# Two made token sums loaded and split in the mixers' temporary tiles, and product 2 of the last up step put last

## The chip, the cores and the metric

One core of one Trainium2 chip runs one launch of the kernel. The metric is the device time of that launch in microseconds, the median of three runs. In the profile, PE is the matrix engine (PEld its weight loads), DVE the vector engine, ACT the scalar engine, POOL and SP two more engines which here mainly issue DMA transfers, each through a queue of its own that works in order.

## The reference

A decoder layer on 2048 tokens of width 1024, all in float32: three kinds of gated token mixers, an output projection into the residual, then an MLP with a causal convolution of width 3.

```python
def conv_ffn(h, w_up, conv_w, conv_b, w_down):
    u = h @ w_up                                   # 1024 -> 2 * 2816
    u = lax.conv_general_dilated(u, ..., feature_group_count=2 * D_FF) + conv_b
    val, gate = jnp.split(u, 2, axis=-1)
    return (jax.nn.silu(gate) * val) @ w_down      # 2816 -> 1024

def reference(x, c, ...):
    ...
        h = rms_norm(x) * (1.0 + sc1) + sh1
        x = x + g1 * token_mixer(h, w_in[l], ..., w_out[l], pos)
        h = rms_norm(x) * (1.0 + sc2) + sh2
        x = x + g2 * conv_ffn(h, w_up[l], conv_w[l], conv_b[l], w_down[l])
    return rms_norm(x) * final_gain
```

## The kernel before

**Numbers.** Every float32 product is made of three matmuls on rounded parts: an operand is split into a high part (a cast on ACT, L1006) and a low part (a subtraction on DVE, L1007) by `split`, and `split3` (L239 to L241) adds high x high, high x low and low x high into one PSUM bank.

**Stages.** The mixers and the output projection go over 4 blocks `b` of 512 tokens. A block's output projection comes in two halves (`out_half`), each of four pieces of weights (`out_piece`, tiles hwo and lwo with block, half and piece in the name); its results are added to the residual x (L953), whose squares (sqn, san) are summed by eight small matmuls (ssn) and brought back to all partitions by eight more (bcn) for the norm n2. The MLP follows in 2 stages `s` of 1024 tokens. The up-projection of a stage (`up_stage`) takes 22 steps `f`, each 128 columns of the value half and of the gate half. A step is one 2 x 2 block product in the form of Winograd and Strassen with 7 products instead of 8: operand A_i comes from the weights, B_i from the tokens, i = 1 to 7. `product(ps, A, B, i, first)` is 4 k-tiles of three matmuls, so 12 matmuls of 128 x 512.

**The order of a step.** `up_first` runs products 1 (bank X), 2 (Y), 6 (X), 5 (Z), 7 (X); ACT copies bank X after 1 (m1), 6 (u2) and 7 (u3), DVE adds Y and Z to uv and ug. `up_second` runs 4 (X) and 3 (Z). Between products 1 and 2 of a step stands `up_second` of the step before, so that copies of X and work of PE overlap; behind the last step `up_second` stands alone.

**The token operands.** B_1, B_2 and B_3 are split from the tokens themselves (hr), B_6, B_5, B_7 and B_4 from sums which `early_sums` makes in DRAM (`made`) while the last block's mixers run. `fetch_made` loads a sum's four k-tiles through POOL into the four `t2k` buffers of the pool "gemm" (tiles hm) and splits them. That pool takes the space that the mixers' pools leave when they are closed. `tmp` gives one of the mixers' six temporary tiles `te`; the split parts of B_7 also live there.

**The weight operands.** A step's A_i are split from loads of up weights (r00, r01, r11: row half and column half) and of their sums (s1 to s4) into the ring `W4` of 1024-wide tiles, which cycles through the buffers that also serve the output weights: whi (3), wlo (3) and wraw (2). The two first products of step 0 of stage 0 are `begun` before the mixers' end, from one 128 x 1024 load (rv0).

**What sets the order.** PE's order is the program's. Other work around it is put into that order by a clock of estimated PE time (`clock.at`): a norm's broadcast is due `gap` after its sums. DVE, ACT, SP and POOL are ordered by a scheduler from the program and its priorities (`tc.high_priority`): each engine then works in order, and an instruction that waits holds up all behind it.

## Time and profile before

| | us |
|---|---|
| median of 3 runs | 2538.81 |
| lowest, highest | 2534.95, 2539.82 |
| the profiled execution | 2537.37 |
| its span | 2535.6 |
| PE busy in it | 2489.7 |
| DVE, ACT, POOL busy | 1949.3, 1136.8, 152.1 |

The span runs from the first to the last instruction that the profile shows. The mean clock granted to PE was 0.992 of the full one. A row of the timeline gives start, duration, engine, line, operation and tiles, and in brackets how long the engine had been idle before it and what released it. Buffer and step numbers are left out in tile names of the profile: X<-B,A is a product of any step.

### The profile page before, as it was taken

What the parts mean: (1) busy time and instruction counts of PE and PEld (TensorE: products, weight loads), DVE (VectorE), ACT (ScalarE), POOL (GpSimd) and SP (SyncE); (2) the same over time, 40 slices, a digit from 0 to 9 for tenths busy, and PEclk for the clock granted to TensorE, in tenths of its full rate; (3) what the DMA queues carried; (4) which work ended last, traced back from release to release, by engine and by line L of the source; (5) the groups of instructions that cost most, each with busy time, mean ns of one, the idle gap of its engine ahead of it and who ended that gap; (6) DMA issues with size and microseconds to landing.
All of it is one profiled execution on the core that took longest, in us unless ns stands there. A gap on an engine that the chain in (4) does not pass through costs nothing.

```text
span 2535.6 us, 37063 instructions
## 1 busy us (share of the span) xinstructions
PE 2489.7 (98%) x13175; PEld 2114.7 (83%) x13175; DVE 1949.3 (77%) x3566; ACT 1136.8 (45%) x1913; POOL 152.1 (6%) x271
## 2 busy tenths in 40 slices
PE   7999999999999999999999999999999999999998
PEld 6898888888789888988788888888877888888887
DVE  8787976869678776868788888877678777778666
ACT  4443434433434335333455554455445545555542
POOL 1000000000000000000100000000001010010000
PEclk9999999999999999999999999999999999999999
DMA  8455575676687846884754544487665544447653
GB/s 295 175 187 175 202 270 209 233 261 215 224 317 266 282 156 240 293 284 142 250 179 149 171 146 145 163 287 240 213 212 169 158 138 153 150 133 259 220 192 126
DMA packets 227930, 524.95 MB, mean 207 GB/s; under 512 B 24952, under 2 KB 28064, under 8 KB 227744
## 3 DMA queue, kind: packets, MB, share of 16 engines
q1 hardware_dynamic: 224544, 512.08, 59.0%
q0 software_dynamic: 3200, 10.49, 1.1%
q8 instruction: 104, 1.70, 0.3%
q14 instruction: 82, 0.67, 0.1%
HBM read 392.97 MB, written 129.50 MB: 206 GB/s over the span
## 4 chain that ended last, share of the span: by engine, by line
PE 58%; DVE 5%; DMA 4%; issue 1%; ACT 1%; SPq 0%; DVEq 0%; ACTq 0%; POOLq 0%
PE X L239 6%; PE X L240 6%; PE X L241 6%; PE Z L240 3%; PE dX L239 3%; PE Z L241 3%; PE dX L240 3%; PE dX L241 3%; PE Z L239 3%; PE Y L239 2%; PE Y L240 2%; PE Y L241 2%; PE dY L239 1%; PE dY L241 1%; PE dY L240 1%
## 5 line engine op out<-in xcount | busy, mean ns | idle before, releaser
L239 PE MATMUL X<-B,A 128*128 128x512 f32 x572 | 223.1, 390 | 1.4 <-ACT u L1285 1.4
L241 PE MATMUL X<-B,A 128*128 128x512 f32 x572 | 222.6, 389 | 0.0
L240 PE MATMUL X<-B,A 128*128 128x512 f32 x572 | 222.6, 389 | 0.0
L1007 DVE TENSOR_TENSOR dA<-rd,dA 128x512 fp32r<-128x512 f32 x154 | 106.0, 688 | 90.5 <-ACT dA L1006 90.1
L1006 ACT CAST dA<-rd 128x512 fp32r<-128x512 f32 x154 | 95.6, 620 | 147.2 <-PE dX L241 62.7
L240 PE MATMUL dX<-dB,dA 128*128 128x512 f32 x396 | 154.3, 390 | 2.7 <-DVE dB L1007 2.7
L239 PE MATMUL dX<-dB,dA 128*128 128x512 f32 x396 | 154.3, 390 | 1.3 <-DVE y L1463 0.9
L241 PE MATMUL dX<-dB,dA 128*128 128x512 f32 x396 | 154.1, 389 | 0.0
L1007 DVE TENSOR_TENSOR A<-s,A 128x512 fp32r<-128x512 f32 x176 | 120.5, 685 | 38.3 <-ACT A L1006 38.1
L239 PE MATMUL psvgh<-hvgh,ha 128*128 128x256 f32 x480 | 141.0, 294 | 0.0
L241 PE MATMUL psvgh<-hvgh,ha 128*128 128x256 f32 x480 | 136.3, 284 | 0.0
L240 PE MATMUL psvgh<-lvgh,ha 128*128 128x256 f32 x480 | 136.2, 284 | 0.0
L1006 ACT CAST A<-s 128x512 fp32r<-128x512 f32 x176 | 108.6, 617 | 53.6 <-PE Z L241 43.5
L239 PEld LDWEIGHTS X<-B,A 128*128 128x128 f32 x572 | 107.4, 188 | 24.4 <-ACT u L1285 2.2
L241 PEld LDWEIGHTS X<-B,A 128*128 128x128 f32 x572 | 107.4, 188 | 22.4
L240 PE MATMUL Z<-B,A 128*128 128x512 f32 x308 | 121.5, 394 | 4.6 <-DVE B L1007 4.6
L240 PEld LDWEIGHTS X<-B,A 128*128 128x128 f32 x572 | 107.4, 188 | 22.2
L643 PE MATMUL lvh<-qbh,kh 128*128 128x128 f32 x896 | 121.9, 279 | 1.5 <-DVE nw L157 1.4
L643 PEld LDWEIGHTS lvh<-qbh,kh 128*128 128x128 f32 x896 | 115.9, 192 | 8.4 <-issue 2.5
L239 PE MATMUL Z<-B,A 128*128 128x512 f32 x308 | 121.0, 393 | 1.2 <-ACT B L1006 1.2
L241 PE MATMUL Z<-B,A 128*128 128x512 f32 x308 | 120.9, 392 | 0.0
L1007 DVE TENSOR_TENSOR dB<-rb,dB 128x512 fp32r<-128x512 f32 x154 | 105.3, 684 | 10.1 <-ACT dB L1006 10.1
(472 smaller groups left out, 6998.9 us busy)
## 6 DMA issues: line engine op xcount, KB each, us to landing
gs<-yv SPq DMA_DIRECT2D x154, 256.0 KB, 2.8
rb<-gs SPq DMA_DIRECT2D x154, 256.0 KB, 4.1
r<-wup SPq DMA_DIRECT2D x141, 256.0 KB, 3.3
s<-sumsu SPq DMA_DIRECT2D x132, 256.0 KB, 3.0
wada<-wada SPq DMA_DIRECT2D x48, 512.0 KB, 4.6
rd<-sumsd SPq DMA_DIRECT2D x88, 256.0 KB, 4.2
rd<-wdown SPq DMA_DIRECT2D x66, 256.0 KB, 3.5
x<-xT SPq DMA_DIRECT2D x64, 256.0 KB, 5.5
```

The source lines that it names most:

```text
L239: T.matmul(ps, lhs[0], rhs[0], start=first, stop=False, skip_group_check=more)
L240: T.matmul(ps, lhs[0], rhs[1], start=False, stop=False, skip_group_check=more)
L241: T.matmul(ps, lhs[1], rhs[0], start=False, stop=last, skip_group_check=more)
L643: T.matmul(ps[:, c * P:(c + 1) * P].rearrange("p (h n s) -> p h n s", h=2, s=s), kq[rs, c * P:(c + 1) * P], rhs, start=True, stop=True)
L1006: S.copy(hi, src)
L1007: V.tensor_tensor(lo, src, hi, op=ALU.subtract)
```

## The change

- The last output piece (block 3, half 1, piece 3) uses the two `wraw` buffers instead of a whi and a wlo.
- The ring `W4` begins with the two `wraw` and then takes whi and wlo in turn; it still has eight places.
- The first up weights come as two 128 x 512 loads (r00, r01) into `te` tiles instead of one into `wraw`.
- Sums 6 and 5 are loaded (`load_made`) right after the first output piece of the last half is begun, into `te` tiles, and split (`split_made`) at a raised priority. Sums 7 and 4 still use `t2k`.
- The due time of the broadcast of the last block's norm n2 goes from 4.5 to 10.0.
- In the last step of either stage product 2 and its sum on DVE (`second`) come behind product 7.
- A parameter `room` is passed through `out_half` and `out_finish`, as None.

```diff
-    def piece(src, name, key, both=False, ahead=50):
+    def piece(src, name, key, both=False, ahead=50, tags=(("whi", 3), ("wlo", 3))):
...
-            hi = pw.tile([P, 1024], F32R, tag="whi", name="h" + name)
-            lo = pw.tile([P, 1024], F32R, tag="wlo", name="l" + name)
+            hi, lo = (pw.tile([P, 1024], F32R, tag=t, name=n + name, bufs=bufs) for n, (t, bufs) in zip("hl", tags))
...
-                     both=True, ahead=250 if (b, half) == (0, 0) else 600 if (b, half) == (NB - 1, 1) else 50)
+                     both=True, ahead=250 if (b, half) == (0, 0) else 600 if (b, half) == (NB - 1, 1) else 50,
+                     tags=[("wraw", NRAW)] * 2 if (b, half, i) == (NB - 1, 1, 3) else (("whi", 3), ("wlo", 3)))
...
-        clock.at(4.0, rstd(acc, f"n2_{b}", bc[:], then if b else lambda: put_off.append(then), gap=8.0 if b < NB - 1 else 4.5))
+        clock.at(4.0, rstd(acc, f"n2_{b}", bc[:], then if b else lambda: put_off.append(then), gap=8.0 if b < NB - 1 else 10.0))
...
-    W4 = [("whi", 3)] * 3 + [("wlo", 3)] * 3 + [("wraw", NRAW)] * 2
+    W4 = [("wraw", NRAW)] * 2 + [("whi", 3), ("wlo", 3)] * 3
...
-    def fetch_made(B, i):
+    def load_made(i, tile):
+        r = []
         for k in range(4):
-            x = t2k(f"hm{i}_{k}")
+            x = tile(f"hm{i}_{k}")
             G.dma_start(x[:], made[i, k][:])
+            r.append(x)
+        return r
+
+    def split_made(B, i, raw):
+        for k, x in enumerate(raw):
             B[i, k] = split(x[:], *hc_tile(f"B0_{i}_{k}"))
...
     with tc.high_priority(offset=300):
-        rv0 = pw.tile([P, 1024], F32, tag="wraw", name="rv0_0", bufs=NRAW)
-        nc.sync.dma_start(rv0[:], wup[0])
         A = {}
-        up_op(A, 0, 0, 1, rv0[:, 0:512])
-        up_op(A, 0, 0, 2, rv0[:, 512:1024])
+        for i in range(2):
+            r = tmp(f"r0{i}_0_0")
+            nc.sync.dma_start(r[:], wup[0][:, 512 * i:512 * i + 512])
+            up_op(A, 0, 0, i + 1, r[:])
...
     with tc.high_priority(offset=100):
         out_begun = [out_begin(NB - 1, 1, 0)]
+        raw6, raw5 = (load_made(i, tmp) for i in (6, 5))
...
-        if not begun:
-            product(Y, A, B, 2, True)
-        with tc.high_priority(offset=HOT):
-            V.tensor_tensor(uv[:, 2:514], Y[:], m1[:], op=ALU.add)
+        def second():
+            if not begun:
+                product(Y, A, B, 2, True)
+            with tc.high_priority(offset=HOT):
+                V.tensor_tensor(uv[:, 2:514], Y[:], m1[:], op=ALU.add)
+        if f < NF - 1:
+            second()
...
             V.tensor_tensor(ug[:, 514:SB + 2], Z[:], u3[:], op=ALU.add)
+        if f == NF - 1:
+            second()
...
-    fetch_made(B, 6)
-    fetch_made(B, 5)
+    with tc.high_priority(offset=100):
+        split_made(B, 6, raw6)
+        split_made(B, 5, raw5)
...
     for i in (7, 4):
-        fetch_made(B, i)
+        split_made(B, i, load_made(i, t2k))
```

POOL's loads of the made sums (hm, sum and k-tile in the name), before:

```order
L1058 DMA hm6_0_12079<-made6_0_9991 128x512
L1058 DMA hm6_1_12084<-made6_1_10301 128x512
L1058 DMA hm6_2_12089<-made6_2_10703 128x512
L1058 DMA hm6_3_12094<-made6_3_11045 128x512
L1265 MEMSET uv0_0_12316 128x2
L1265 MEMSET ug0_0_12317 128x2
L1265 MEMSET uv0_1_12421 128x2
L1058 DMA hm5_0_12099<-made5_0_9988 128x512
L1058 DMA hm5_1_12104<-made5_1_10298 128x512
L1058 DMA hm5_2_12109<-made5_2_10700 128x512
L1058 DMA hm5_3_12114<-made5_3_11042 128x512
L1058 DMA hm7_0_12251<-made7_0_9994 128x512
```

The same twelve places now:

```order
L1059 DMA hm6_0_12040<-made6_0_9991 128x512
L1059 DMA hm6_1_12042<-made6_1_10301 128x512
L1059 DMA hm6_2_12044<-made6_2_10703 128x512
L1059 DMA hm6_3_12046<-made6_3_11045 128x512
L1059 DMA hm5_0_12048<-made5_0_9988 128x512
L1059 DMA hm5_1_12050<-made5_1_10298 128x512
L1059 DMA hm7_0_12253<-made7_0_9994 128x512
L1059 DMA hm7_1_12255<-made7_1_10304 128x512
L1059 DMA hm7_2_12257<-made7_2_10706 128x512
L1059 DMA hm5_2_12052<-made5_2_10700 128x512
L1059 DMA hm5_3_12054<-made5_3_11042 128x512
L1059 DMA hm7_3_12259<-made7_3_11048 128x512
```

The loads of sum 5 move ahead of the three memsets, and three of sum 7 ahead of sum 5's last two.

DVE around the end of the last mixer (oTr) and the first sum of step 0 (uv), ahead of the last block's residual updates (x1), before:

```order
L1278 TENSOR_TENSOR uv0_0_12316<-Y0_0_11989,m1_0_0_12320 128x512
L587 SCALAR_TENSOR_TENSOR oTr3_1_12043<-oTr3_1_12038,vec_84,oTr3_1_12043 128x512
L1007 TENSOR_TENSOR B0_6_0_12081<-hm6_0_12079,B0_6_0_12081 128x512
L1007 TENSOR_TENSOR B0_6_1_12086<-hm6_1_12084,B0_6_1_12086 128x512
L953 SCALAR_TENSOR_TENSOR x1_3_0_11636<-y3_1_0_12018,mod_102,x1_3_0_11636 128x512
L953 SCALAR_TENSOR_TENSOR x1_3_0_11636<-y3_1_1_12019,mod_102,x1_3_0_11636 128x512
L953 SCALAR_TENSOR_TENSOR x1_3_2_11751<-y3_1_2_12050,mod_102,x1_3_2_11751 128x512
L953 SCALAR_TENSOR_TENSOR x1_3_2_11751<-y3_1_3_12051,mod_102,x1_3_2_11751 128x512
```

Now:

```order
L1286 TENSOR_TENSOR uv0_0_12318<-Y0_0_11991,m1_0_0_12322 128x512
L1007 TENSOR_TENSOR B0_6_0_12097<-hm6_0_12040,B0_6_0_12097 128x512
L1007 TENSOR_TENSOR B0_6_1_12100<-hm6_1_12042,B0_6_1_12100 128x512
L1007 TENSOR_TENSOR B0_6_2_12103<-hm6_2_12044,B0_6_2_12103 128x512
L1007 TENSOR_TENSOR B0_6_3_12106<-hm6_3_12046,B0_6_3_12106 128x512
L1007 TENSOR_TENSOR B0_5_0_12109<-hm5_0_12048,B0_5_0_12109 128x512
L1007 TENSOR_TENSOR B0_5_1_12112<-hm5_1_12050,B0_5_1_12112 128x512
L586 SCALAR_TENSOR_TENSOR oTr3_1_12061<-oTr3_1_12056,vec_84,oTr3_1_12061 128x512
L1007 TENSOR_TENSOR lB0_7_0_12262<-hm7_0_12253,hB0_7_0_12261 128x512
L1007 TENSOR_TENSOR B0_5_2_12115<-hm5_2_12052,B0_5_2_12115 128x512
```

Eight low parts of sums (L1007) stand ahead of the residual updates instead of two; the third and fourth of sum 6 and all of sum 5 stood behind them.

SP's loads for the last half's output pieces (hwo, lwo) and the first up steps (r, s), before:

```order
L223 DMA lwo3_1_0_12015<-kepto4l_3461 128x1024
L223 DMA lwo3_1_1_12047<-kepto5l_3522 128x1024
L222 DMA hwo3_1_0_12014<-kepto4h_3459 128x1024
L223 DMA lwo3_1_2_12150<-kepto6l_3577 128x1024
L222 DMA hwo3_1_1_12046<-kepto5h_3520 128x1024
L222 DMA hwo3_1_2_12149<-kepto6h_3575 128x1024
L1199 DMA s1_0_0_12192<-sumsu0_11589 128x512
L1199 DMA s0_0_0_12191<-sumsu0_11589 128x512
L1138 DMA r11_0_0_12207<-wup 128x512
L1138 DMA r00_0_1_12383<-wup 128x512
L1138 DMA r01_0_1_12385<-wup 128x512
L1138 DMA r11_0_1_12409<-wup 128x512
```

Now:

```order
L1119 DMA r00_0_0_11980<-wup 128x512
L1119 DMA r01_0_0_11985<-wup 128x512
L221 DMA hwo3_1_0_12016<-kepto4h_3459 128x1024
L222 DMA lwo3_1_0_12017<-kepto4l_3461 128x1024
L221 DMA hwo3_1_1_12064<-kepto5h_3520 128x1024
L222 DMA lwo3_1_1_12065<-kepto5l_3522 128x1024
L221 DMA hwo3_1_2_12151<-kepto6h_3575 128x1024
L222 DMA lwo3_1_2_12152<-kepto6l_3577 128x1024
L221 DMA hwo3_1_3_12189<-kepto7h_3639 128x1024
L222 DMA lwo3_1_3_12190<-kepto7l_3641 128x1024
L1206 DMA s1_0_0_12194<-sumsu0_11589 128x512
L1206 DMA s0_0_0_12193<-sumsu0_11589 128x512
```

The output pieces stand together, the last of them now ahead of the first sums of up weights (s1, s0) instead of behind them, and the two loads of the first up weights stand at the head.

More of the change, by code (lines that the diff above doesn't have):

```diff
@@ L939, in out_begin, with out_half @@
         return wp, pss
-    def out_half(b, half, acc=None, after_pieces=None, begun=()):
+    def out_half(b, half, acc=None, after_pieces=None, begun=(), room=None):
         for i in range(4):
@@ L955, in out_half, with out_finish @@
                     with tc.high_priority(offset=HOT):
-                        sumsq(acc, x1[m], m, f"n2_{b}_")
+                        sumsq(acc, x1[m], m, f"n2_{b}_", room=room)
     put_off = []
-    def out_finish(b, after_pieces=None, begun=()):
+    def out_finish(b, after_pieces=None, begun=(), room=None):
         acc = new_acc(f"n2_{b}")
-        out_half(b, 1, acc, after_pieces, begun)
+        out_half(b, 1, acc, after_pieces, begun, room)
         rows = list(x1)
@@ L1481, in trunk @@
     with tc.high_priority(offset=100):
-        out_finish(NB - 1, lambda: up_weights(0, 0, A), out_begun)
+        out_finish(NB - 1, lambda: up_weights(0, 0, A), out_begun, None)
     for i in (7, 4):
-        fetch_made(B, i)
+        split_made(B, i, load_made(i, t2k))
     for k in range(4):
```

## The prediction

> **What bounds the kernel now.** I read the page first, then the waits of TensorE, then windows and timelines around each wait that the change touches. The page and the waits:

> ```profile
> span 2535.6 us, 37063 instructions
> PE 2489.7 (98%) x13175; PEld 2114.7 (83%) x13175; DVE 1949.3 (77%) x3566; ACT 1136.8 (45%) x1913; POOL 152.1 (6%) x271
> PE Z L240 <- DVE B L1007: 4.6, 5, 3.0
> PE X L239 <- ACT u L1285: 1.4, 2, 0.7
> ```

> TensorE is busy for 98% of the span and the change issues the same matmuls, so it can only gain where TensorE stands still or runs slowly, 46 us in all for the standing. A line of waits gives total, count and longest. The largest that the change touches is one stall of 3.0 us, product 5 (into bank Z) waiting for a split token sum. What that stall costs is more than its length:

> ```profile
> 1235.00:1240.00 5.00, 5.00 (x24) 4.14 (x23) 2.80 (x5) 2.95 (x6) 0.00 (x0) 1.00 0.91 318
> 1240.00:1245.00 5.00, 2.00 (x9) 1.36 (x8) 4.85 (x8) 2.87 (x6) 0.54 (x1) 0.98 0.77 225
> 1245.00:1250.00 5.00, 5.00 (x16) 3.74 (x15) 2.36 (x10) 0.33 (x1) 1.61 (x3) 0.50 0.71 265
> 1250.00:1255.00 5.00, 4.70 (x11) 3.21 (x11) 3.39 (x9) 2.83 (x6) 2.14 (x4) 0.50 0.49 164
> 1255.00:1260.00 5.00, 5.00 (x27) 4.22 (x27) 4.24 (x7) 4.58 (x10) 0.58 (x1) 1.00 0.62 217
> ```

> Each row is a stretch with busy time of PE, PEld, DVE, ACT and POOL, then granted clock and DMA share. The clock is 0.50 in two whole rows after the row with the hole. The matmuls themselves:

> ```profile
> 1237.85 0.39 PE L239 MATMUL X<-B,A 128*128 128x512 f32 x1
> 1240.57 0.39 PE L239 MATMUL Z<-B,A 128*128 128x512 f32 x1
> 1243.96 0.50 PE L240 MATMUL Z<-B,A 128*128 128x512 f32 x1 [3.00 <-DVE B L1007]
> 1250.34 0.79 PE L239 MATMUL X<-hB,A 128*128 128x512 f32 x1 [0.30 <-ACT hB L1006]
> 1256.26 1.05 PE L327 MATMUL bcn<-c_all,rsn 128*128 128x128 f32 x8
> 1257.07 0.47 PE L239 MATMUL X<-B,A 128*128 128x512 f32 x1
> 1265.52 0.50 PE L240 MATMUL Z<-B,A 128*128 128x512 f32 x1 [0.57 <-DVE B L1007]
> 1266.09 0.39 PE L239 MATMUL Y<-B,A 128*128 128x512 f32 x1
> ```

> A product of 12 matmuls takes 1240.57 − 1237.85 = 2.72 us. From 1240.57 to 1266.09 stand five products and two groups of eight small matmuls (the sums and the broadcast of the norm; 1257.07 − 1256.26 = 0.81 us each at full clock). Undisturbed that is 5 x 2.72 + 2 x 0.81 = 15.2 us; it takes 25.5. So **10.3 us** are lost here: 3.2 in the stall (1243.96 − 1240.57, less one spacing of 2.72/12 = 0.227); 0.3 at 1250.34; 1.5 behind 1257.07, from where 33 matmuls (7.5 us) take the 9.0 to 1266.09, with the 0.57 among them; and the rest, 5.3, to the half clock.

> **Why the sum is late.** POOL issues the loads of the made sums in order, four buffers deep, and ACT and DVE stand still meanwhile:

> ```profile
> 1203.02 0.68 POOL L1058 DMA_DIRECT2D hm<-made  x1 [61.30 <-PE scr L872]
> 1208.61 1.60 POOL L1058 DMA_DIRECT2D hm<-made  x3 [4.92 <-issue]
> 1222.69 1.14 POOL L1058 DMA_DIRECT2D hm<-made  x2 [12.26 <-DVE B L1007]
> 1232.71 1.14 POOL L1058 DMA_DIRECT2D hm<-made  x2 [8.89 <-ACT sqn L337]
> 1213.14 0.59 ACT L1272 COPY m<-X 128x512 f32<-128x512 f32 x1 [2.99 <-PE X L241]
> 1220.32 0.69 ACT L586 ACTIVATE oTr<-oTr,vec 128x512 fp32r<-128x512 f32 x1 [6.58 <-PE oTr L583]
> 1220.90 2.17 ACT L1006 CAST B<-hm 128x512 fp32r<-128x512 f32 x4
> 1215.86 0.69 DVE L1278 TENSOR_TENSOR uv<-Y,m 128x512 f32<-128x512 f32 x1 [0.52 <-PE Y L241]
> 1221.04 0.75 DVE L587 SCALAR_TENSOR_TENSOR oTr<-oTr,vec,oTr 128x512 fp32r<-128x512 f32 x1 [4.49 <-ACT oTr L586]
> 1243.22 1.28 DVE L1007 TENSOR_TENSOR B<-hm,B 128x512 fp32r<-128x512 f32 x2
> ```

> The first six loads are issued by 1223.8, the last two of sum 5 only at 1232.71; its first two low parts run on DVE at 1243.22, behind operands and squares, where TensorE wanted them at 1240.8. Before that, ACT was idle 6.58 us and DVE 4.49 us with no sum in hand.

> **Part 1, sums 6 and 5 loaded and split early.** Six of the eight loads now go at once to `te` tiles that the mixers have let go, and need no buffer of the `gemm` pool, for which POOL waits till 1203 above. By what they wait for in the new order they can be issued between 1190 and 1198, when the DMA engines carry little (share 0.15 in the first row below). POOL issues take 0.54 us each (1.60 for 3), landing 3.7 us, so all six lie ready by 1203. In the new order of ACT and DVE their splits follow m and uv directly: casts from 1213.7 at some 0.54 us (2.17 for four), low parts from 1216.5 at some 0.62 us (1.28 for two): six end at 1220.3, inside the idle 4.49 us. Sum 5's other two wait for the first two low parts of sum 6 (1217.7), land 3.7 us later near 1222 and are split by about 1230: 10 us ahead of 1240.57. The A operands of these products are loaded by SP:

> ```profile
> 1190.00:1200.00 10.00, 10.00 (x68) 9.10 (x67) 9.25 (x24) 3.89 (x8) 0.00 (x0) 1.00 0.15 54
> 1216.15 0.91 SPq L1199 DMA_DIRECT2D s<-sumsu  x2
> 1228.44 0.69 DVE L1007 TENSOR_TENSOR A<-s,A 128x512 fp32r<-128x512 f32 x1
> hm<-made POOLq DMA_DIRECT2D x16, 256.0 KB, 3.7
> ```

> On SP, in order, the weight sums s1, s0 now stand behind the last output piece, whose two `wraw` buffers come free with the first two up products near 1215.6, and wait themselves for buffers that the last transposes free at 1220.3: 4.2 us later than 1216.15. A6's low part then moves from 1228.44 to about 1232.6 and A5's to about 1235, still 5 us before product 6 at 1237.85. So the stall of 3.2 goes, and with it what triggers the half clock.

> Behind it DVE's whole queue is shorter by the eight splits, and the casts of sum 7 come off loads issued before 1200 instead of after 1244; the 0.30 wait goes too. Walking the new orders with landings of 3.3 us, the norm's sums are there 0.8 us before TensorE asks, the copy u3 1.2 us before, and the last of B3 just in time at about 1255. I keep 0.5 us of the 1.5 behind 1257.07 as still lost. The step is worth 10.3 − 0.5 = 9.8; bounds 6.1 (waits of 3.7 us in place of the old ones, and the half clock gone; rival A has their parts) and 10.3.

> On the clock: one stall of 3.0 us brought two full rows at 0.50 here. [...]

> **Part 2, first up weights in two halves through `te` tiles.** One SP load at 1145 becomes two near 1188, after the low parts that free their tiles.

> ```profile
> 1187.89 0.68 DVE L1007 TENSOR_TENSOR B<-hr_0a,B 128x512 fp32r<-128x512 f32 x1
> 1191.26 0.68 DVE L1007 TENSOR_TENSOR A<-rv,A 128x512 fp32r<-128x512 f32 x1
> 1194.20 0.61 PE L583 MATMUL oTh<-c_all,oh 128*128 128x128 f32 x4
> r<-wup SPq DMA_DIRECT2D x141, 256.0 KB, 3.3
> ```

> Issued at 1188.6, landed 3.3 later, cast 0.6: A1's low part can begin about 1191.9 instead of 1191.26, A2's now stands in the same stretch, and oh behind them ends some 0.6 later than TensorE's transposes at 1194.20 like. Cost 0.3, bounds 0 and 1.0. The added SP issue (0.3 us) and the other halves of the W4 ring cost nothing: eight buffers, reused after eight operands, as before.

> **Part 3, product 2 of the last step moved behind product 7, both stages.**

> ```profile
> 1657.55 0.39 PE L241 MATMUL X<-hB,A 128*128 128x512 f32 x1
> 1658.62 0.50 PE L239 MATMUL X<-B,A 128*128 128x512 f32 x1 [0.68 <-ACT u L1285]
> 1666.80 0.50 PE L239 MATMUL dX<-dB,dA 128*128 128x512 f32 x1 [0.40 <-DVE uv L1236]
> ```

> Product 4 accumulates into the bank that ACT is still copying: 1658.62 − 1657.55 − 0.227 = 0.84, and the first matmul takes 0.11 more than 0.39: 0.95 us. The row of waits (1.4 in two) holds the same gap of the other stage. Product 2 has its own bank and 2.72 us, which cover the copy (over just before 1658.62). Products 6, 5 and 7 come 2.72 us earlier; their operands were cast well before (ACT had turned to down operands). The 0.40 at 1666.80 may grow by 0.5, since its evacuation sits in DVE's queue. I take 0.9 per stage, 1.8; bounds 0.9 and 1.9.

> **Part 4, broadcast of the norm 24 matmuls later:** 0.81 us wherever it stands; it then waits for nothing. Nothing, bounds 0 and 0.3.

> **Sum:** 9.8 − 0.3 + 1.8 = 11.3 us. The profiled execution took 2537.4, 1.4 less than the median 2538.8; so 2526.1 by the one, **2527.5** against the median.

> One thing is outside the sum: four gaps at the start of stage 1 also bring a half clock.

> ```profile
> 1904.46 0.50 PE L239 MATMUL Z<-B,A 128*128 128x512 f32 x1 [1.23 <-ACT B L1006]
> 1908.00:1913.00 5.00, 4.68 (x11) 3.71 (x12) 5.00 (x9) 1.86 (x2) 1.63 (x3) 0.50 0.80 254
> ```

> Its second row shows five slow microseconds, 11 matmuls where 22 would fit: 2.5 us lost. Whether such a stretch comes can change with the shift of 11 us and from run to run: ±2.5 on any case.

> **Rivals.** *A, the stall is passed on* (0.20). ACT takes casts and copies in order. In the new order the copy u3, which frees the bank for product 4, stands behind casts of A1_5, A1_7 and B4 that wait for SP and POOL loads issued after 1238. If these land in 5 us instead of 3.3, as they may at the DMA share of 0.91 of 1235 to 1240, I count 1.0 us before the norm's sums, 2.2 before product 4, 0.5 in product 3. Alone: 2531. Spread over a few us as at 1904, they bring back 2.5 us of half clock: 2538.8 − 11.3 + 3.7 + 2.5 = 2534. For it: sum 4's loads wait for sum 7's low parts. Against: DMA is relieved between 1210 and 1240, since output pieces load from 1190.

> *B, slower* (0.10): SP's queue. r00 waits for a tile at SP's head, the last output piece behind it for the first up products, s1 for the transposes; s2, s3 and step 1's loads follow. Spare is 5.2 us at A6 (1232.6 against 1237.85). If the s loads slip by 10 us more, product 6 stalls 4.8 at 1237.85, product 5 another 2.4 (A5 is that far behind A6), products 7 and 4 the 3.7 of A, and the clock is halved once more as now, 5.3: 16.2, less the 11.3 gives +4.9, 2544. With the other three terms it is slower than before from a slip of about 6 us on. For it: DVE and ACT do these splits between residual updates, and a late one pushes the next. Against: the order itself adds 4.2 us of slip, and SP has nothing else to wait for.

> *C, the change doesn't do what it says* (0.08): hm5's last two loads, on POOL behind sum 7's, come so late that product 5 still stalls 3 us; only part 3 counts: 2537.

> **How the numbers follow.** Forecast 0.62, around 2527.5 with its own range 2523 to 2532. About 5 us is what a measurement of this kernel can tell from no change (0.2%), so it counts as faster, as does nearly half of A; the rest of A, C and a part of B as same: faster 0.72, same 0.20, slower 0.08. The range 2523 to 2536 takes in A.

> **What would show it.** After: no wait of Z L240 above 0.6 us before 1260; clock 1.00 in every row from 1235 to 1265; casts of B right behind m at 1213; the first Y matmul of step 1 near 1256.5; no wait on the u copy of the last steps; oTh within 1 us of 1194.2. It is wrong if the clock still shows 0.50 there, or a new wait above 2 us stands at X.

## The result, and the profile after

The changed kernel takes 2525.06 us (median of 4 runs, 2523.43 to 2525.66), the kernel before 2539.32 us (median of 4). The ratio is 0.9955, 95% interval 0.9944 to 0.9967. A second series gave 2526.35 us and 0.9954 (0.9936 to 0.9972). Against 2538.8 us the ratio means 11.4 us less, where 11.3 were forecast; the medians alone lie 14.3 apart, in the second series 13.5. The ratio with its interval is the measured one of a series; the quotient of the two medians can lie up to 0.0011 lower, as here (0.9944).

First the page and the waits of TensorE after the change (total, count, longest):

```profile
span 2523.6 us, 37047 instructions
PE 2481.0 (98%) x13175; PEld 2110.3 (84%) x13175; DVE 1945.3 (77%) x3566; ACT 1135.4 (45%) x1913; POOL 159.7 (6%) x271
PE X L238 <- ACT u L1295: 1.7, 2, 1.1
PE Z L239 <- DVE B L1007: 1.6, 4, 0.8
```

The span is 12.0 us shorter, and TensorE's busy time 8.7 us: the same matmuls ran at half clock for less time (from 1215 to 2505 us 17.07 us before, 10.24 from 1244.80 and 6.83 from 1906.98, and none after). The 3.0 us wait for a split sum is gone; the 1.6 that are left are all at the start of stage 1. New is a wait for the copy u3. The same windows as before:

```profile
1240.00:1245.00 5.00, 5.00 (x28) 4.22 (x26) 4.18 (x8) 3.13 (x6) 0.54 (x1) 1.00 0.75 224
1245.00:1250.00 5.00, 5.00 (x24) 4.17 (x25) 4.06 (x11) 2.43 (x5) 1.06 (x2) 1.00 0.90 303
1250.00:1255.00 5.00, 3.90 (x18) 2.88 (x17) 3.88 (x11) 3.78 (x8) 0.57 (x1) 1.00 0.66 225
```

The granted clock, third number from the right, is 1.00 in every row; the third row holds the hole of the new wait. TensorE's timeline there and at the mixers' end:

```profile
1196.04 0.63 PE L582 MATMUL oTh<-c_all,oh 128*128 128x128 f32 x4 [0.29 <-DVE oh L576]
1240.18 0.39 PE L238 MATMUL X<-B,A 128*128 128x512 f32 x1
1249.02 0.39 PE L240 MATMUL X<-hB,A 128*128 128x512 f32 x1
1253.23 0.50 PE L238 MATMUL X<-B,A 128*128 128x512 f32 x1 [1.10 <-ACT u L1295]
1256.80 1.05 PE L326 MATMUL bcn<-c_all,rsn 128*128 128x128 f32 x8
1259.77 0.39 PE L238 MATMUL Y<-B,A 128*128 128x512 f32 x1
1293.17 0.50 PE L238 MATMUL X<-B,A 128*128 128x512 f32 x1 [0.59 <-ACT u L1295]
1894.16 0.51 PE L238 MATMUL Z<-B,A 128*128 128x512 f32 x1 [0.46 <-ACT B L1006]
```

From the first matmul of product 6 in step 0 to the first of product 2 in step 1 it is 1259.77 − 1240.18 = 19.6 us. Before it was 28.2, from 1237.85 (12 matmuls ahead of the 1240.57 of the prediction) to 1266.09. This stretch, called **the boundary** below, is the measure of nearly all experiments. DVE and ACT now split the sums in their idle time:

```profile
1196.78 3.25 POOL L1059 DMA_DIRECT2D hm<-made  x6 [0.67 <-DVE B L1007]
1215.96 1.14 ACT L1006 CAST B<-hm 128x512 fp32r<-128x512 f32 x2
1218.80 3.69 DVE L1007 TENSOR_TENSOR B<-hm,B 128x512 fp32r<-128x512 f32 x6
1233.87 0.68 DVE L1007 TENSOR_TENSOR A<-s,A 128x512 fp32r<-128x512 f32 x1
1252.07 0.62 ACT L1006 CAST B<-hm 128x512 fp32r<-128x512 f32 x1 [1.21 <-DMA hm<-made]
1252.60 0.58 ACT L1295 COPY u<-X 128x512 f32<-128x512 f32 x1
```

Six low parts run in one piece from 1218.80. A6's low part begins at 1233.87, 6.3 us ahead of product 6. The last two rows are the late copy u3: product 7 had filled its bank with the matmul of 1249.02, but ACT comes to the copy at 1252.60, behind a cast of sum 4 that waited 1.21 us for its load.

### The profile page after: what moved, and what is told of

Its sections match the earlier page's. It is cut to its first block, busy times and chain, and to the rows that moved or that the text cites. A ratio compares the mean times of both kernels' runs of the same rounds, so it can differ in the third digit from the quotient of the medians.

```text
span 2523.6 us, 37047 instructions
## 1 busy us (share of the span) xinstructions
PE 2481.0 (98%) x13175; PEld 2110.3 (84%) x13175; DVE 1945.3 (77%) x3566; ACT 1135.4 (45%) x1913; POOL 159.7 (6%) x271
## 5 line engine op out<-in xcount | busy, mean ns | idle before, releaser
L239 PE MATMUL X<-B,A 128*128 128x512 f32 x572 | 222.6, 389 | 0.0
L240 PE MATMUL X<-B,A 128*128 128x512 f32 x572 | 222.5, 389 | 0.0
L1007 DVE TENSOR_TENSOR dA<-rd,dA 128x512 fp32r<-128x512 f32 x154 | 105.9, 689 | 90.4 <-ACT dA L1006 90.2
L1006 ACT CAST dA<-rd 128x512 fp32r<-128x512 f32 x154 | 95.5, 621 | 143.8 <-PE dX L240 57.3
L239 PE MATMUL dX<-dB,dA 128*128 128x512 f32 x396 | 154.2, 389 | 1.7 <-DVE dB L1007 1.7
L240 PE MATMUL dX<-dB,dA 128*128 128x512 f32 x396 | 154.1, 389 | 0.0
L1007 DVE TENSOR_TENSOR A<-s,A 128x512 fp32r<-128x512 f32 x176 | 120.5, 685 | 38.6 <-ACT A L1006 38.5
L1006 ACT CAST A<-s 128x512 fp32r<-128x512 f32 x176 | 108.6, 618 | 69.8 <-PE Z L240 40.3
L240 PE MATMUL psvgh<-hvgh,ha 128*128 128x256 f32 x480 | 136.4, 284 | 0.0
L239 PE MATMUL psvgh<-lvgh,ha 128*128 128x256 f32 x480 | 136.3, 284 | 0.0
L240 PEld LDWEIGHTS X<-B,A 128*128 128x128 f32 x572 | 107.4, 188 | 22.4
L239 PEld LDWEIGHTS X<-B,A 128*128 128x128 f32 x572 | 107.4, 188 | 22.2
L239 PE MATMUL Z<-B,A 128*128 128x512 f32 x308 | 120.3, 390 | 1.6 <-DVE B L1007 1.6
L240 PE MATMUL Z<-B,A 128*128 128x512 f32 x308 | 119.8, 389 | 0.0
L1007 DVE TENSOR_TENSOR A<-r,A 128x512 fp32r<-128x512 f32 x132 | 90.5, 686 | 26.4 <-ACT A L1006 26.1
## 6 DMA issues: line engine op xcount, KB each, us to landing
gs<-yv SPq DMA_DIRECT2D x154, 256.0 KB, 2.8
rb<-gs SPq DMA_DIRECT2D x154, 256.0 KB, 4.0
r<-wup SPq DMA_DIRECT2D x143, 256.0 KB, 3.3
s<-sumsu SPq DMA_DIRECT2D x132, 256.0 KB, 3.0
rd<-sumsd SPq DMA_DIRECT2D x88, 256.0 KB, 4.0
rd<-wdown SPq DMA_DIRECT2D x66, 256.0 KB, 3.8
x<-xT SPq DMA_DIRECT2D x64, 256.0 KB, 5.3
```

The lines of the kernel that those rows point to most:

```text
L239: T.matmul(ps, lhs[0], rhs[1], start=False, stop=False, skip_group_check=more)
L240: T.matmul(ps, lhs[1], rhs[0], start=False, stop=last, skip_group_check=more)
L1006: S.copy(hi, src)
L1007: V.tensor_tensor(lo, src, hi, op=ALU.subtract)
```

## The experiments

Times of one kernel vary by up to 9 us about their median (run 4), so most of the reading goes by the boundary in each kernel's trace, where the matmuls are the same 60 + 12 and 16 small ones. Each boundary is that of one profiled execution. All measured values (before, changed, then runs 1 to 10 in order):

| kernel | boundary, us | waits of TensorE in it | median, us | ratio to before (95%) |
|---|---|---|---|---|
| before | 28.2 | B 3.0, half clock | 2539.32 | |
| changed, 1st and 2nd profile | 19.6, 19.0 | u3 1.1, 0.3 | 2525.06, 2526.35 | 0.9955 (0.9944 to 0.9967), 0.9954 (0.9936 to 0.9972) |
| sums late again | 26.0 | B 1.9, half clock | 2533.91 | 0.9982 (0.9972 to 0.9993) |
| old weight buffers | 21.2 | san 1.2, half clock (short) | 2524.41 | 0.9945 (0.9932 to 0.9958) |
| broadcast early again | 25.9 | rsn 4.9, half clock | 2530.08 | 0.9972 (0.9961 to 0.9983) |
| before + last step | 28.4 | B 3.4, half clock | 2536.61 | 0.9996 (0.9983 to 1.0009) |
| before + broadcast late | 28.9 | B 3.5, half clock | 2537.42 | 0.9991 (0.9982 to 1.0000) |
| before + early sums | 28.9 | rsn 6.9, half clock | 2536.31 | 0.9994 (0.9984 to 1.0005) |
| old buffers, norm's sums later | 20.5 | u3 2.6 | 2526.08 | 0.9949 (0.9936 to 0.9961) |
| sums 7 and 4 raised by 100 | 25.4 | A 4.4, half clock | 2534.88 | 0.9982 (0.9970 to 0.9993) |
| by 160 and 60 | 18.5 | none above 0.2 | 2527.55 | 0.9951 (0.9937 to 0.9966) |
| the same, old buffers | 18.8 | san 0.2 | 2528.20 | 0.9955 (0.9939 to 0.9970) |

**1. Sums 6 and 5 late again**, the rest of the change kept.

```diff
-        raw6, raw5 = (load_made(i, tmp) for i in (6, 5))
...
-    with tc.high_priority(offset=100):
-        split_made(B, 6, raw6)
-        split_made(B, 5, raw5)
+    for i in (6, 5):
+        split_made(B, i, load_made(i, t2k))
```

> The changed kernel, but sums 6 and 5 are again loaded into the t2k buffers after the mixers and split in program order; all else of the change stays. Theory (the early load and split is what removes the stall and the half clock): the wait of product 5 for its split sum is back at 2 us or more, the granted clock falls to 0.50 for some 10 us behind it, and the time rises by 7 to 10 us, to 2532 to 2535, ratio to before about 0.998. Rival (the weight buffers and the order of SP's loads bring the gain, since the DMA engines are relieved between 1210 and 1240): sum 5 comes in time here too and the time rises by less than 2 us, ratio about 0.996.

The windows of this kernel at the boundary:

```profile
1250.00:1255.00 5.00, 3.06 (x15) 2.21 (x13) 3.90 (x7) 3.27 (x7) 0.54 (x1) 1.00 0.94 302
1255.00:1260.00 5.00, 5.00 (x18) 4.33 (x19) 3.38 (x12) 0.68 (x2) 2.15 (x4) 0.60 0.78 227
1260.00:1265.00 5.00, 4.91 (x16) 3.00 (x15) 3.46 (x10) 2.25 (x4) 1.98 (x4) 0.72 0.60 171
```

The stall (1.94 us) and the half clock (6.8 us of it) are back, both somewhat shorter than the theory had them. The boundary is 6.4 us longer than in the changed kernel, and 2533.91 us lies in the range that the theory gave, well past the rival's 2 us. The early sums are needed. That they do it by themselves this run does not say.

**2. The weight buffers as before**: tags of the last output piece, order of W4, one load rv0.

```diff
-    W4 = [("wraw", NRAW)] * 2 + [("whi", 3), ("wlo", 3)] * 3
+    W4 = [("whi", 3)] * 3 + [("wlo", 3)] * 3 + [("wraw", NRAW)] * 2
...
-                     tags=[("wraw", NRAW)] * 2 if (b, half, i) == (NB - 1, 1, 3) else (("whi", 3), ("wlo", 3)))
+                     tags=(("whi", 3), ("wlo", 3)))
...
-        for i in range(2):
-            r = tmp(f"r0{i}_0_0")
-            nc.sync.dma_start(r[:], wup[0][:, 512 * i:512 * i + 512])
-            up_op(A, 0, 0, i + 1, r[:])
+        up_op(A, 0, 0, 1, rv0[:, 0:512])
+        up_op(A, 0, 0, 2, rv0[:, 512:1024])
```

> The changed kernel, but the last output piece, the ring W4 and the one load of the first up weights are as before; early sums, broadcast and last step stay changed. Theory: only the late transposes of oh (1.1 us between 1194 and 1198) come back, so it is 1 us faster than the changed kernel, 2524, ratio to before about 0.995; no stall above 0.6 us at product 5. Rival (the buffers carry part of the gain): the output pieces load late again, the DMA engines are crowded from 1210 to 1240, and product 5 or 7 waits 2 us or more: 2528 to 2535.

2524.41 us, not to be told from the changed kernel. Its trace:

```profile
1241.47 1.02 PE L316 MATMUL ssn<-c_all,san 128*128 128x1 f32 x8 [1.22 <-DVE san L337]
1240.00:1245.00 5.00, 3.78 (x18) 3.04 (x17) 5.00 (x13) 2.96 (x6) 0.54 (x1) 0.81 0.90 302
1245.00:1250.00 5.00, 5.00 (x21) 4.04 (x20) 3.06 (x8) 3.03 (x6) 0.00 (x0) 0.85 0.88 290
```

Neither account was whole. Product 5 does not stall, as the theory said. But the norm's sums wait 1.22 us and the clock dips, so that the boundary is 1.6 us longer than in the changed kernel; in return oh is on time and the wait at 1293 does not come. The two sides cancel: that the new buffers bring anything in all is not shown.

**3. The broadcast at its old place**, the rest of the change kept: `gap` 4.5 instead of 10.0.

> The changed kernel with the due time of the last norm's broadcast at 4.5 again, so that its eight matmuls stand 24 matmuls earlier. The prediction's term: it waits for nothing in either place, 0 to 0.3 us, 2525. Rival, read from the changed kernel's trace: rsn is complete there only at 1255.4, while the old place is reached at about 1250, so TensorE waits some 5 us in front of the broadcast and then runs at half clock for 7 to 10 us: 7 to 11 us slower than the changed kernel, 2532 to 2536.

```profile
1256.44 2.05 PE L326 MATMUL bcn<-c_all,rsn 128*128 128x128 f32 x8 [4.93 <-DVE rsn L158]
1250.00:1255.00 5.00, 1.51 (x7) 0.93 (x5) 3.55 (x11) 3.26 (x7) 0.00 (x0) 1.00 0.84 270
1255.00:1260.00 5.00, 3.56 (x13) 3.21 (x14) 4.05 (x9) 2.49 (x6) 0.57 (x1) 0.50 0.36 111
1260.00:1265.00 5.00, 5.00 (x20) 4.04 (x19) 3.48 (x6) 3.25 (x6) 0.00 (x0) 0.81 0.33 120
```

Rows of this kernel's timeline and windows. The eight matmuls of the broadcast wait 4.93 us for rsn and the clock halves. The boundary takes 25.9 us, 6.3 more than the 19.6. The rival holds in its mechanism; by the medians the loss is 4 to 5 us, and both figures lie below its range of 7 to 11. A term that the prediction had at nothing is worth as much at the boundary as the early sums (6.3 against 6.4 us); by the medians it is worth about half as much (4 to 5 against 8 to 9).

**4. The last step alone, on the kernel before.**

> The kernel before with nothing changed but product 2 of the last step put behind product 7, in both stages. Theory: the wait of 0.68 us for the copy u at the end of each stage goes, 0.9 us each, and nothing comes for it: 1.8 us faster than before (1.6 to 2.6), ratio about 0.9993. Rival: the evacuations that it delays let the down projection's first banks wait as long: 0 us, ratio 1.000.

The two waits for u (1658.62 and 2304.00 before) are not in this trace. From product 2 of step 1 to the first matmul of the down projection of stage 0 it takes 397.14 us, where the kernel before takes 398.10: 1.0 us in stage 0, as forecast. The time, 2.6 us shorter by medians, cannot tell 1.8 from nothing (interval 0.9983 to 1.0009).

**5 and 6. The late broadcast alone, and the early sums alone, on the kernel before.** These two complete the square of sums and broadcast.

> The kernel before with nothing changed but the due time of the last norm's broadcast, 10.0 instead of 4.5. Theory (the stall of 3 us and the half clock cover the norm's chain there, so the broadcast waits for nothing): no change, ratio 1.000 within 0.1%. Rival (the later broadcast is a gain or a loss by itself): more than 2 us either way.

> The kernel before with the early load and split of sums 6 and 5 alone; broadcast, buffers and last step as before. The prediction's sum: 9.8 us faster. Rival, from the run with the broadcast at 4.5: the stall is passed on to the broadcast, which waits 4 to 5 us for rsn and brings the half clock back, so that only 1 to 4 us are gained: 2535 to 2538, ratio 0.9985 to 0.9995.

Neither has any effect that shows: 28.9 us each at the boundary, against 28.2. The time of the second, 2536.31 us, is where its rival had it. With the sums alone TensorE stands still again, at another place:

```profile
1257.83 2.04 PE L327 MATMUL bcn<-c_all,rsn 128*128 128x128 f32 x8 [6.85 <-DVE rsn L158]
1250.00:1255.00 5.00, 0.98 (x5) 0.48 (x3) 2.23 (x6) 2.42 (x5) 0.00 (x0) 0.83 0.74 256
1255.00:1260.00 5.00, 2.17 (x9) 2.20 (x10) 4.67 (x11) 2.54 (x6) 0.57 (x1) 0.50 0.38 112
```

The stall for B is gone there, and the 6.85 us for rsn take its place. In the kernel before, the old stall and its half clock gave the norm's chain on DVE the time that it needs. There the chain (L320 to the last L158) runs from 1247.31 to 1253.11, 3.2 us ahead of the broadcast. With the sums alone its eleven instructions of some 0.16 us run from 1246.39 to 1257.68, between splits that wait for ACT's casts, and TensorE is there by 1251. Only the two edits together bring the gain: neither 28.2, broadcast 28.9, sums 28.9, both 21.2 (old buffers) or 19.6 (new ones).

**7. Toward a faster kernel: the norm's sums later**, in the kernel with the old buffers (`clock.at(6.5, ...)` for the last block instead of 4.0).

> The run with the old weight buffers, and in it the last norm's sums due at 6.5 instead of 4.0, so that its eight matmuls and the broadcast behind them stand 2.5 us later. The trace of that run shows TensorE waiting 1.22 us for san in front of the sums, and the clock at 0.81 and 0.85 in the two rows there. Theory: both go and nothing comes for them, 1.2 + 1.7 us: 2.5 to 3 us faster than that run, ratio to before 0.9935. Rival: the whole chain behind it (u3, B4, B3) is what comes late, and the wait is only passed on to product 4: ratio 0.9945, no change.

2526.08 us, ratio 0.9949 (0.9936 to 0.9961). The wait for san is gone, the boundary 20.5 us instead of 21.2, but the rival has it: product 4 now waits 2.60 us for u3.

**8 to 10. Sums 7 and 4 at raised priority**: in the changed kernel by 100 both; by 160 and 60; and the latter with the old weight buffers. A second profile of the changed kernel went with them.

```diff
     for i in (7, 4):
-        split_made(B, i, load_made(i, t2k))
+        with tc.high_priority(offset=160 if i == 7 else 60):
+            split_made(B, i, load_made(i, t2k))
```

> The changed kernel once more, for a second profile and more times. From the first: product 6 to product 2 of the next step 19.6 us, with a wait of about 1.1 us in front of product 4; ratio to before 0.995 to 0.996. If the half clock at the start of stage 1, seen in the profile of before alone, is a matter of chance, it may appear here.

> The changed kernel, and in it the loads and splits of sums 7 and 4 at a priority raised by 100, as those of 6 and 5. The copy u3 then stands on ACT ahead of the casts of A1_5 and A1_7 and behind all of B4, whose loads POOL can issue some 10 us earlier. Theory: the wait of 1.1 us in front of product 4 goes, product 6 to product 2 takes 18.0 to 18.5 us instead of 19.6, ratio to before 0.995. Rival: the splits of sum 4 now stand between the squares of the last norm on DVE and ACT, and TensorE waits as long in front of the norm's sums: no change or 1 us slower.

> As the run before, but with sum 7 raised by 160 and sum 4 by 60, so that fewer splits stand between the squares. Theory: the wait for u3 goes and the norm's sums are not late: 18.0 to 18.5 us from product 6 to product 2, 1.1 to 1.6 us faster than the changed kernel. Rival: as in the run before, the wait moves to the norm's sums.

> The same priorities (160 and 60) with the old weight buffers. The run with those buffers had no late oh, and in front of product 4 no wait, but waited 1.22 us in front of the norm's sums. Theory: that wait stays or grows, since the splits of sum 7 come on top: 20 to 21.5 us from product 6 to product 2, ratio to before 0.9945. Rival: with sum 7 split early the later queue is shorter and the wait goes: 18.5 us, ratio 0.9935.

The second profile of the changed kernel shows a boundary of 19.0 us, a wait of 0.32 us in front of product 4 where 1.1 was expected, and no half clock at the start of stage 1; the times of that series go from 2524.47 to 2534.03 us. With 100 the kernel loses most of the gain: 2534.88 us, ratio 0.9982 (0.9970 to 0.9993), boundary 25.4 us. From its trace:

```profile
1246.31 0.79 PE L240 MATMUL X<-B,A 128*128 128x512 f32 x1 [4.43 <-DVE A L1007]
1229.01 0.62 ACT L1006 CAST A<-s 128x512 fp32r<-128x512 f32 x1 [2.51 <-PE y L239]
1241.86 1.28 DVE L1007 TENSOR_TENSOR B<-hm,B 128x512 fp32r<-128x512 f32 x2
1245.57 0.68 DVE L1007 TENSOR_TENSOR A<-s,A 128x512 fp32r<-128x512 f32 x1
```

A6 was cast at 1229.01, but its low part runs at 1245.57, behind the splits of sums 4 and 7, for some of which ACT's casts wait 0.77 to 1.87 us for loads; product 6 waits 4.43 us for it. Both expectations missed this place: the wait is not at the norm's sums but one product earlier. With 160 and 60 the boundary falls to 18.5 us as the theory has it, near the 17.9 that it takes without any wait (2.72 + 15.2), but the gain goes elsewhere: 2527.55 us, ratio 0.9951 (0.9937 to 0.9966), since step 1 now waits for its own u3:

```profile
1294.15 0.50 PE L238 MATMUL X<-B,A 128*128 128x512 f32 x1 [1.98 <-ACT u L1295]
```

With the old buffers the boundary is 18.8 us, as that run's rival had it, but not the time that it gave (ratio 0.9935): 2528.20 us, ratio 0.9955 (0.9939 to 0.9970). None of these is shown to beat the changed kernel.

## Why the prediction was right, point by point

**The total** came out as forecast: the ratio is 0.9955, and 2527.5/2538.8 is 0.9955. By stretches, the changed one minus the one before: 8.6 us gained at the boundary; 2.3 lost ahead of it (1.4 of them by the transposes qTr at 1181.93, ahead of all that the change moved but the load rv0; in the 13 profiles they stand anywhere from 1177.96 to 1192.32); nothing between step 1 and the end of stage 0's up steps (398.11 against 398.10 us); 1.8 gained in the down projection, untouched too; 4.5 gained in the up steps of stage 1. These sum to 12.5 at the last matmul. Of the signs that the prediction named, the clock, the wait of product 5 and the waits of the last steps came as it said. Two did not: the first Y matmul of step 1 stands at 1259.77 and not near 1256.5, and oTh at 1196.04, 1.8 us behind 1194.2 and not within 1.

**The early sums** removed the stall and the half clock, for the reason that was given: six of the eight loads issued by 1200, splits right behind m and uv, the last of sum 5 ahead of need. The 9.8 us were measured as 8.6, and 9.3 in the second profile, since 1.1 and 0.3 us of rival A came true at its place, product 4 behind u3. Its half clock did not come.

**The broadcast** is the step that failed: "0.81 us wherever it stands; it then waits for nothing. Nothing". The move was priced at nothing, but without the stall the broadcast waits for nothing only in its new place. At the old one it costs 6.3 us of the boundary (run 3), and without it the early sums bring nothing (run 6). The walk of the orders behind the 9.8 had the broadcast at its new place, so the sum was right and the credit wrong. What I had not asked is what else the old stall was hiding.

**The first up weights** cost 0.3 to 0.9 us, where 0.3 was given with an upper bound of 1.0: from the transposes qTr (1181.93) to those of oh (1196.04) it is 14.1 us, where the kernel before takes 13.65 (from 1180.55 to 1194.20), and from there to product 6 it is 44.1 instead of 43.65. So 0.9 us in this profile, with a wait of 0.29 for oh from DVE in it. The second profile and runs 1 and 3, which have the new loads too, take 13.65 and 44.0 to 44.1 us, so 0.3 to 0.4; the run with the old buffers has 43.65 again.

**The last step** removed both waits for u as forecast (run 4: 1.0 us in stage 0). In the changed kernel stage 0 does not show the gain, for a wait of 0.59 us at step 1 eats it: there u3 stands on ACT behind a cast that waited 4.85 us for a sum of up weights. Run 2 has no such wait, but run 10, with the old buffers too, has one of 0.56 us, so that the new buffers alone bring it is not shown.

**The DMA relief** that spoke against rival A came where the prediction had it, from 1210 to 1240 (mean share 0.72, before 0.89), but not behind it: from 1245 to 1250 the share is 0.90, before 0.71, and there the loads of sum 4 are late.

**Luck** had a part in the profile: the half clock at the start of stage 1, which the prediction left out of its sum with ±2.5, is in the profile of before (0.62 to 0.70 around 1908) and not in those of the changed kernel; of the other ten, only the one of run 8 (priority 100) shows it, behind a first gap of 1.29 us. The two rows of 5 us from 1905 to 1915 (0.70 and 0.62) show that it lasted 6.8 us and cost 3.4, not the 2.5 that the prediction read from one row. With the last step's 0.9 this is nearly all of the 4.5 us of stage 1. So of the 12.5 us between the two profiles some 5 (3.4, and 1.8 in the down projection) stand where the sum had nothing, and what it did name brought some 7 of its 11.3. That the ratio gives 11.4 is in part luck.

Rivals B and C have no trace in the result: A5 and A6 were ready in time, 6.3 us for A6, and hm5's last two loads too.

## What to carry to other kernels

A stall on the bound engine gives time to everything else that is late; before removing it, ask which chain is next and by how much, and remove both, or neither edit shows a gain. Undo each part of a change alone and do it alone: here two edits are worth nothing each and 7 to 9 us together. When a wait is passed on from place to place as in runs 7 to 10, look at the stretch behind the one that improved before calling it a gain.

## What the runs showed of the hardware that was not expected

In these runs the length of a stall alone did not decide whether the clock halved. These are windows of two kernels, before with the late broadcast (first two) and with the norm's sums later:

```profile
1753.00:1758.00 5.00, 1.97 (x10) 1.32 (x9) 3.46 (x6) 2.70 (x5) 0.00 (x0) 1.00 0.50 190
1758.00:1763.00 5.00, 5.00 (x24) 4.14 (x23) 5.00 (x9) 1.62 (x3) 0.00 (x0) 1.00 0.49 138
1255.00:1260.00 5.00, 2.40 (x11) 1.68 (x10) 3.42 (x10) 3.56 (x7) 0.57 (x1) 1.00 0.51 187
1260.00:1265.00 5.00, 5.00 (x26) 4.22 (x26) 4.87 (x14) 2.89 (x6) 0.00 (x0) 1.00 0.31 109
```

```profile
1239.69:1243.10 3.41, 2.19 (x14) 1.70 (x13) 3.40 (x7) 2.66 (x6) 0.00 (x1) 1.00 0.89 269
1243.10:1246.51 3.41, 3.41 (x9) 2.65 (x8) 2.33 (x8) 0.62 (x1) 0.54 (x1) 0.50 1.02 332
1246.51:1249.93 3.42, 3.42 (x16) 2.82 (x15) 2.56 (x6) 2.96 (x6) 0.00 (x0) 1.00 0.83 288
1253.52:1256.93 3.41, 1.99 (x9) 1.31 (x7) 1.13 (x4) 1.11 (x2) 0.00 (x0) 1.00 0.93 330
1256.93:1260.35 3.42, 2.24 (x10) 1.86 (x11) 3.26 (x9) 3.42 (x8) 0.57 (x1) 1.00 0.24 93
```

The whole stall of run 2 lies in one step, together with the norm's eight sums of a single column each. The longer stall of run 7 is divided between two steps, and neither is followed by half clock.

Take 0.227 us for every 512 columns that a matmul streams, the spacing measured at full clock, and call the rest of a step empty. In run 2 the step with the stall has 2.36 us empty, in run 7 the two have 1.59 and 1.31. In the kernel before, the steps ahead of its two slow stretches have 2.70 us (from 1241.38) and 2.09 (from 1903.57). In the kernels before and changed, from 1215 to 2505 us, the emptiest step at full clock with no half clock behind it has 1.96 (from 1862.61, before). These figures were counted after the runs, and no run set where the steps begin, so whether the empty time decides is not shown.
